# Queries and keys of the forgetting heads by one level of Strassen, late values with tokens stationary, and an inverse rms spread by DMA

## The chip, the cores and the metric

The kernel runs on one core of one Trainium2 chip. The metric is the device time of one execution in microseconds (us); the time before is the median of three runs. The core has five engines that each take their own instructions in order: TensorE (PE in the profile, its weight loads apart as PEld), VectorE (DVE), ScalarE (ACT), GpSimd (POOL) and SyncE (SP). SP computes nothing here; it issues nearly all DMAs, one after the other, and an issue that must wait for a buffer holds those behind it. Engines wait for each other by semaphores.

## The reference, cut to what matters

One layer over 1024 tokens of width 1024, in float32. The part that the change touches is the input projection and what feeds from it:

```python
h = rmsnorm(x, g_mix_pre[l])
proj = h @ w_in[l]                      # 1024 x 3080
fq, fk, fv = ...                        # 8 forgetting heads of 64: 512 columns each
f_logit = proj[..., 1536:1544] + b_fgt  # one forget gate per forgetting head
cq, ck, cv = ...                        # 8 chunked heads of 64: 512 columns each
# forgetting attention: causal softmax of q.k/8 + cumulative sum of log sigmoid(f_logit)
# chunked attention: own chunk of 64 and 8 chunks before, with a relative bias
x = x + rmsnorm(concat(rmsnorm(y_fox), rmsnorm(y_chk)) @ w_out, g)
x = x + rmsnorm(memory_cross_attention(rmsnorm(x), rmsnorm(mem), w_mq, w_mk, w_mv, w_mo), g)
x = x + rmsnorm(square(relu(rmsnorm(x) @ w_ff1)) @ w_ff2, g)
```

## The kernel before

**Arithmetic.** Every float32 operand of a product is held as two rounded tiles, a high part (hi, the operand rounded by an ACT copy) and a low part (lo, operand minus hi, on DVE or POOL). A product is three matmuls, hi by hi, hi by lo, lo by hi (mm3, L174 to L176). The gain of the norm is multiplied into x^T when it is split (hT, L1590); the inverse rms of a token is multiplied in after the projection, from a tile rt that holds it along the free dimension, the same in all 128 partitions.

**Stages.** The opening (L1522 to L1709) is written out by hand in one order for all engines. Slabs of x^T for the first 512 tokens (half th=0) land together with 264 columns of value and gate weights (xw, L1542); as each lands, it is split and multiplied into the values of the first four forgetting heads, tokens stationary (value_rounds, L1633). Then come the values of the other forgetting heads, the second half of the tokens, and beside them the rms: the rows of x are squared on ACT with a running sum (L1600), POOL adds epsilon and takes the power -1/2 (root), DVE spreads that over a diagonal matrix (L1610, L1612), PE multiplies it with ones and ACT copies the result out as rt (spread, L1619, L1621). After the last value part the forget gates are worked out on DVE and ACT (forget_gates, L392 to L426), transposed on PE (ftr), summed by a scan on DVE (L424), and stored; the bias rows of the attention are loaded from there.

The attention (attention_phase) is laid out by a planner (Flow, L56 to L126). It holds streams of steps: values (pv), turns (transposes ptr), scores (sc), side steps, row norms, and last a filler. Step by step it takes the first stream whose next step has its operands and buffers by its own reckoning, and it orders DVE, ACT, POOL and the DMAs by due time and level. What it decides is fixed when the program is built. The filler (filler_steps, L1492) runs, for the eight pairs of heads (four forgetting, n=0 to 3, then four chunked, n=4 to 7), the projections of queries and keys with weights stationary, 512 tokens wide (project_steps, L681): a scaling by rt on DVE (L724), splits per head, and for keys copies by DMA to the other 64 partitions (L746). For chunked pairs it also makes values (vt) with weights stationary, which PE transposes later (vtr, L762 on). After these come the memory keys, the first half of the output projection (mix_steps(0)) and the memory values. Beside the planner, pumps issue loads when buffers come free: Stock (L262) the weights, Biases (L434) the bias rows, WeightSums (L913) loads w_mo during the attention, forms four differences of its blocks on DVE (L926) and stores them in DRAM (wt) for the memory's output projection, which already runs as a Strassen product. The feed-forward part after it (lines from L1709 on, with Block, HiLo, bank and product as helpers) does so too.

## Time and profile before

| what | value |
|---|---|
| median of 3 runs | 1453.06 us (1452.79 to 1455.76) |
| span of the profiled execution | 1451.2 us (the page prints no other time of it) |
| mean granted TensorE clock | 0.999 |
| opening, 0 to 60 us: PE, DVE, ACT, POOL busy | 58.95, 29.82, 40.65, 17.22 us; 225 GB/s |
| attention with projections, 60 to 440 us | 380.00, 279.57, 251.43, 179.56 us; 143 GB/s |
| attention, output projection and memory queries, 440 to 700 us | 259.52, 173.85, 160.17, 50.87 us; 183 GB/s |
| the rest, 700 us to the end | 744.92, 479.36, 371.01, 136.33 us; 192 GB/s |

A matmul is pipelined: its busy time in the profile (0.28 to 0.39 us) is longer than the step from one start to the next. What one costs is read from the starts. In lines of a timeline the columns are start, time, engine, line, operation, tiles (written <- read), shape and count; in brackets stands the idle time before and what ended it. Lines of waits end in three numbers: the sum, the count, the mean. A group line gives the busy time, the mean of one in ns, and the idle time before with its releasers. A line of DMA issues gives their count, the KB of each, and the median us from issue to landing.

### The profile page before, as it was taken

How to read it: one execution, taken by the hardware profiler on the slowest of the kernel's cores; microseconds unless marked ns; L12 is line 12 of the kernel's file. 1: busy time of each engine (PE TensorE's matmuls, PEld its weight loads, DVE VectorE, ACT ScalarE, POOL GpSimd, SP SyncE). 2: the span in 40 equal slices, each digit the busy share in tenths (PEclk: the TensorE clock that was granted, in tenths of full speed). 3: DMA queues.
4: the chain of work that ended last, by engine and by line, in shares of the span. 5: the costliest groups of instructions: out<-in, count | busy, mean ns of one | idle time of the engine just before them, and what ended most of it. 6: DMA issues, size and time to landing. Idle time of an engine off the chain costs nothing.

```text
span 1451.2 us, 20902 instructions
## 1 busy us (share of the span) xinstructions
PE 1443.4 (99%) x7252; PEld 1222.7 (84%) x7252; DVE 962.6 (66%) x1651; ACT 823.3 (57%) x1466; POOL 384.0 (26%) x454
## 2 busy tenths in 40 slices
PE   9999999999999999999999999999999999999998
PEld 9988888888889888888888888888888888888886
DVE  5567778867667546966685697655555766655576
ACT  7457776676577664566665455545555453444442
POOL 1345555444344102400021504333331000000021
PEclk9999999999999999999999999999999999999999
DMA  8233667854548766542352646754444775445565
GB/s 335 66 102 91 146 166 191 279 120 124 134 95 247 216 204 237 188 161 63 123 200 74 211 154 231 264 185 159 160 160 160 297 304 192 138 148 189 185 250 203
DMA packets 100970, 259.44 MB, mean 179 GB/s; under 512 B 12520, under 2 KB 25072, under 8 KB 100864
## 3 DMA queue, kind: packets, MB, share of 16 engines
q1 hardware_dynamic: 96112, 249.71, 51.3%
q0 software_dynamic: 4608, 8.39, 4.0%
q8 instruction: 57, 0.93, 0.3%
q14 instruction: 49, 0.40, 0.1%
q10 hardware_dynamic: 144, 0.00, 0.0%
HBM read 181.98 MB, written 76.08 MB: 178 GB/s over the span
## 4 chain that ended last, share of the span: by engine, by line
PE 98%; DVE 0%; DMA 0%; ACT 0%; issue 0%; SPq 0%; DVEq 0%; POOLq 0%; POOL 0%; ACTq 0%
PE pv L638 4%; PE fx L175 4%; PE fx L174 4%; PE fx L176 4%; PE ptr L588 4%; PE px L176 3%; PE fy L174 3%; PE px L175 3%; PE fy L175 3%; PE px L174 3%; PE fy L176 3%; PE yw L174 2%; PE q L174 2%; PE q L176 2%; PE q L175 2%; PE mq L174 2%
## 5 line engine op out<-in xcount | busy, mean ns | idle before, releaser
L594 DVE TENSOR_TENSOR p<-ptr,p 128x512 fp32r<-128x512 f32 (+1 forms) x152 | 92.5, 616 | 29.4 <-ACT p L597 28.5
L2102 ACT ACTIVATE whif<-ra 128x1024 fp32r<-128x1024 f32 x37 | 39.2, 1061 | 126.2 <-PE fy L175 62.6
L2104 DVE TENSOR_TENSOR wlof<-ra,whif 128x1024 fp32r<-128x1024 f32 x37 | 45.3, 1225 | 88.7 <-ACT whif L2102 88.7
L597 ACT ACTIVATE p<-ptr 128x512 fp32r<-128x512 f32 (+1 forms) x152 | 79.9, 538 | 41.7 <-PE ptr L588 40.8
L2216 POOL TENSOR_SCALAR rf<-sf 128x1 f32<-128x1 f32 x8 | 8.2, 1030 | 324.7 <-ACT jf L2201 324.5
L638 PE MATMUL pv<-p,vs 128*128 128x512 f32 (+1 forms) x304 | 86.3, 371 | 0.0
L174 PE MATMUL fx<-vhif,whif 128*128 128x512 f32 x168 | 65.4, 389 | 0.0
L176 PE MATMUL fx<-vhif,wlof 128*128 128x512 f32 x168 | 65.4, 389 | 0.0
L175 PE MATMUL fx<-vlof,whif 128*128 128x512 f32 x168 | 65.4, 389 | 0.0
L638 PEld LDWEIGHTS pv<-p,vs 128*128 128x128 f32 x304 | 53.4, 189 | 8.7 <-DVE p L594 0.2
L1991 POOL TENSOR_TENSOR sc<-wf,wf 128x512 f32<-128x512 f32 x14 | 21.7, 1553 | 144.1 <-DMA wf<-in_w_ff 144.1
L174 PE MATMUL k<-hT_hi,whik 128*128 128x512 f32 x128 | 52.6, 411 | 0.0
L174 PE MATMUL mq<-h2T_hi,whimq 128*128 128x512 f32 x128 | 51.6, 403 | 0.0
L174 PE MATMUL q<-hT_hi,whiq 128*128 128x512 f32 x128 | 51.0, 398 | 0.0
L174 PE MATMUL yw<-whiwo,yT_hi 128*128 128x512 f32 x128 | 50.6, 395 | 0.0
L175 PE MATMUL k<-hT_lo,whik 128*128 128x512 f32 x128 | 50.2, 393 | 0.0
L176 PE MATMUL k<-hT_hi,wlok 128*128 128x512 f32 x128 | 50.2, 392 | 0.0
L176 PE MATMUL q<-hT_hi,wloq 128*128 128x512 f32 x128 | 50.1, 391 | 0.0
L176 PE MATMUL mq<-h2T_hi,wlomq 128*128 128x512 f32 x128 | 50.1, 391 | 0.0
L175 PE MATMUL q<-hT_lo,whiq 128*128 128x512 f32 x128 | 50.1, 391 | 0.0
L175 PE MATMUL mq<-h2T_lo,whimq 128*128 128x512 f32 x128 | 50.0, 391 | 0.0
L176 PE MATMUL yw<-whiwo,yT_lo 128*128 128x512 f32 x128 | 49.9, 390 | 0.0
(673 smaller groups left out, 4941.1 us busy)
## 6 DMA issues: line engine op xcount, KB each, us to landing
ra<-gd SPq DMA_DIRECT2D x56, 512.0 KB, 3.7
wg<-in_w_ff SPq DMA_DIRECT2D x56, 512.0 KB, 5.0
wf<-in_w_ff SPq DMA_DIRECT2D x38, 512.0 KB, 4.0
gd<-s SPq DMA_DIRECT2D x48, 256.0 KB, 2.1
od<-ot SPq DMA_DIRECT2D x64, 128.0 KB, 2.7
od<-od POOLq DMA_DIRECT2D x32, 256.0 KB, 4.9
wrawmq<-in_w_mq SPq DMA_DIRECT2D x16, 512.0 KB, 3.9
gd<-u SPq DMA_DIRECT2D x32, 256.0 KB, 2.0
```

The costliest lines, as they stand in the source:

```text
L174: nc.tensor.matmul(ps, lh, rh, start=start, stop=False, skip_group_check=more)
L175: nc.tensor.matmul(ps, lh, rl, start=False, stop=False, skip_group_check=more)
L176: nc.tensor.matmul(ps, ll, rh, start=False, stop=stop, skip_group_check=more)
L588: nc.tensor.transpose(tr[:, m, :], sp[:, k * P:(k + 1) * P], ident)
L594: flow.put("V", at, 0.56 if dead else 0.7, lambda: nc.vector.tensor_sub(pl[:, live, :], tr[:, live, :], f(ph[:, live, :])), done)
L597: flow.put("S", flow.end, 0.49 if dead else 0.6, lambda ph=ph, tr=tr, live=live: nc.scalar.activation(ph[:, live, :], tr[:, live, :], AF.C ...
L638: nc.tensor.matmul(pv[:, :, q0 * P:(q0 + k1 - k0) * P], v, x[:, :, k0:k1, :].rearrange("p m k q -> p m (k q)"), start=c == 0 and m == 0, s ...
L1991: eng.tensor_sub(sc[:, k1], r0[:, k0], r1[:, k0])
L2102: nc.scalar.activation(ah, ra, AF.Copy)
L2104: nc.vector.tensor_sub(al, ra, f(ah))
L2216: nc.gpsimd.tensor_scalar(r, ssf[b][:, 0:1], ssf[b][:, 1:2], EPS, op0=ALU.add, op1=ALU.add)
```

## The change

**Queries and keys of the four forgetting pairs move into the opening (NS = 4).** With x^T cut into quarters, B11 and B21 (first 512 tokens, first and second half of the width) and B12 and B22 (the second 512 tokens), and the weights of one pair into four blocks (query and key, first and second half of the width), the four result blocks (query and key, each for two halves of tokens) are made of seven products instead of eight, each 12 matmuls of 128x512. Two of the seven need only raw weights and first-half slabs: the slabs now bring the query weights of all four pairs (x_wq0, L1544), and as they land the products with B11 (firsts) and B21 (seconds) run, 12 matmuls for each slab (L1628). The first goes to DRAM, as does the sum of both, named g11 (second_out, L1602 to L1606, tiles part1). The other operands are sums of quarters of the normed x^T: POOL norms (L1609), DVE forms T1 and T2 (L1660, L1661), POOL T3 and T4, and `turned` splits T2, T1, T3, T4 and B22 (L1654, L1655). The rows of x have two buffers now, and the square of one issues the load of the row two behind (L1582). Then a class Pair loads a pair's raw query and key weights (wq, wk, L1560), forms three weight sums sc, r1 and sd (L1725 to L1729), on DVE for the first pair and on POOL for the others, and splits them (L205, L208; tiles v, w and u, with s23, s1a and s4 in their names). Per pair five products follow (x with T2, z with T1, x with T3, v with T4, z with B22), and `emit` multiplies by rt, splits and stores a query's or key's hi and lo half to DRAM (qkd, L1768 to L1779). The attention loads them from there, three tiles of a head by six DMAs (class Heads, L530).

**The values of the forgetting heads come after the pairs.** B12 is loaded again and split (L1856 to L1861), the value weights come in their own loads (w_v0, w_v1), and four value parts follow, all their matmuls as before. Between them stand the weight differences of w_mo (weight_sums replaces WeightSums), the gates, their transposes, scan and store, which were side steps before, the first loads of queries and keys, and the first bias rows.

**The inverse rms is spread by DMA.** `root` stores the 512 inverse rms of a half as 512 elements in DRAM (rdr, L1591) and loads them back to all partitions (rt0, rt1, L1592). The diagonal, its matmuls and the copy go.

**Late values with tokens stationary.** The values of the chunked pairs are made two pairs at a time, 256 columns wide and tokens stationary (late_value_steps), without transposes. Projections of the chunked pairs (project_steps) store their halves in DRAM too. Memory values stand ahead of mix_steps(0) in the filler, and buffer counts and levels of the planner follow.

Three places show how instructions move; the number at the end of a name is a running number of the tile. On SP, at the end of the opening's loads, there stood before the last rows of x, two small loads, and the first query and key weights of the attention:

```order
L1562 DMA x_4_397<-in_x 128x1024 [waits DMAHW5_49,Activation_49]
L1562 DMA x_5_399<-in_x 128x1024 [waits DMAHW6_49,Activation_49]
L1562 DMA x_6_401<-in_x 128x1024 [waits DMAHW7_49,Activation_49]
L1562 DMA x_7_403<-in_x 128x1024 [waits DMAHW0_49]
L1678 DMA bfgt_85<-in_b_fgt 128x8 [waits DMAHW1_49]
L1679 DMA gcol_86<-in_g_heads 128x8 [waits DMAHW2_49]
L310 DMA wrawq_0_407<-in_w_qk 128x1024 [waits DMAHW3_49,DVE_49]
L310 DMA wrawk_0_409<-in_w_qk 128x1024 [waits DMAHW4_49,DVE_49]
```

Now, from the last store of part1 to the weights of the first pair:

```order
L1605 DMA part1_3_147<-xw7_216 128x512 [waits DMAHW1_49]
L1606 DMA part1_3_147<-g11_3_453 128x512 [waits DMAHW2_49,DVE_49]
L1554 DMA x_5_474<-in_x 128x1024 [waits DMAHW3_49,Activation_49]
L1554 DMA x_6_477<-in_x 128x1024 [waits DMAHW4_49,Activation_49]
L1591 DMA rdr_143<-rall_88 128x4x1 [waits DMAHW5_49,Pool_49]
L1592 DMA rt0_89<-rdr_143 128x512 [waits DMAHW6_49,DMAHW5_49]
L1554 DMA x_7_496<-in_x 128x1024 [waits DMAHW7_49,Activation_49]
L1560 DMA wq0_512<-in_w_qk 128x1024 [waits DMAHW0_49]
L1560 DMA wk0_514<-in_w_qk 128x1024 [waits DMAHW1_49]
```

The two weight loads stood behind rows of x before as well; now the stores, the write of the inverse rms and its load back stand among the rows, with waits for DVE, ACT and POOL, and wq0 and wk0, which the first pair's products need, stand behind all of them.

On ACT, from the squares of the second half of the rows on, there stood the value copies (vs), the copy of rt, and the high part of the first query weight of the attention:

```order
L1600 ACTIVATE junk6_609,ss41_222<-x_6_401 128x1024 [waits DMAHW7_49,Activation_49]
L1600 ACTIVATE junk7_611,ss41_222<-x_7_403 128x1024 [waits DMAHW0_49,Activation_49]
L1647 ACTIVATE vs1_0_201<-v100_245,rall_88 128x4x64
L1647 ACTIVATE vs1_0_201<-v101_246,rall_88 128x4x64
L1621 ACTIVATE rt1_671<-rt1_668 128x512 [waits PE_49]
L323 ACTIVATE whiq_0_779<-wrawq_0_407 128x1024 [waits DMAHW3_49]
L323 ACTIVATE whik_0_784<-wrawk_0_409 128x1024 [waits DMAHW4_49]
```

Now, from the square of x_5 (two splits of T4 and one of B22 are left out here):

```order
L1582 ACTIVATE x_5_474,ss41_243<-x_5_474 128x1024 [waits DMAHW3_49,Activation_49]
L1582 ACTIVATE x_6_477,ss41_243<-x_6_477 128x1024 [waits DMAHW4_49,Activation_49]
L1582 ACTIVATE x_7_496,ss41_243<-x_7_496 128x1024 [waits DMAHW7_49,Activation_49]
L1654 ACTIVATE T4_hi0_500<-xw4_210 128x512 [waits Pool_49]
L1654 ACTIVATE T4_hi1_501<-xw7_216 128x512 [waits Pool_49]
L1654 ACTIVATE hT1k2_hi0_238<-xt12_220 128x512 x2
L1654 ACTIVATE hT1k2_hi1_239<-xt13_224 128x512
L205 ACTIVATE vhi_s230_542<-qsc0_534 128x1024 [waits DMAHW5_49,DVE_49,Activation_49]
L205 ACTIVATE whi_s1a0_546<-wk0_514 128x1024 [waits DMAHW1_49]
```

The splits of T4 and B22 stand between the squares and the first pair's weight split vhi_s230, which the first product of that pair, PE's row after the slab products, reads.

On DVE, around the start of the gates (fz is the gate's logit), the value parts' low halves were followed by the gates at once:

```order
L1650 SCALAR_TENSOR_TENSOR vs0_2_199<-v010_533,rall_88,vs0_2_199 128x4x64 [waits PE_49,Activation_49]
L1650 SCALAR_TENSOR_TENSOR vs0_3_200<-v013_536,rall_88,vs0_3_200 128x4x64 [waits PE_49,Activation_49]
L397 TENSOR_TENSOR fz_773<-fcol_144,bfgt_85 128x8 [waits DMAHW1_49]
L397 TENSOR_TENSOR fz_773<-fcol_144,bfgt_85 128x8 x7
L401 TENSOR_SCALAR fl_775<-fz_773 128x64 [waits DVE_49]
```

Now the second four differences of w_mo stand ahead of the last value part's low halves and of the gates:

```order
L948 TENSOR_TENSOR wm111_1099<-wm121_1100,wm111_1099 128x1024 [waits DMAHW6_49,DMAHW5_49]
L948 TENSOR_TENSOR wm121_1100<-wm221_1102,wm121_1100 128x1024 [waits DMAHW7_49,DVE_49]
L948 TENSOR_TENSOR wm221_1102<-wm221_1102,wm111_1099 128x1024 [waits DVE_49]
L948 TENSOR_TENSOR wm211_1101<-wm211_1101,wm221_1102 128x1024 [waits DMAHW0_49,DVE_49]
L1892 SCALAR_TENSOR_TENSOR vs0_2_1085<-v010_1236,rall_88,vs0_2_1085 128x4x64 [waits PE_49,Activation_49]
L1892 SCALAR_TENSOR_TENSOR vs0_3_1086<-v013_1239,rall_88,vs0_3_1086 128x4x64 [waits PE_49,Activation_49]
L429 TENSOR_TENSOR fz_1348<-fcol_1082,bfgt_85 128x8 [waits DMAHW2_49]
L429 TENSOR_TENSOR fz_1348<-fcol_1082,bfgt_85 128x8 x7
L433 TENSOR_SCALAR fl_1350<-fz_1348 128x64 [waits DVE_49]
```

All eight differences left the attention for this place, each with waits for its own loads.

The diff, cut to its core:

```diff
+    NS = 4
+    VS = {5: 2, 7: 3}
...
-    class WeightSums:
...
+    def weight_sums(k):
+        raw = {n: u4(f"wm{n}{k}", (P, 2, HT), F32) for n in ("11", "12", "21", "22")}
+        for n, (a, b) in (("12", (0, 1)), ("11", (0, 0)), ("22", (1, 1)), ("21", (1, 0))):
+            nc.sync.dma_start(raw[n], mo(a, b, k))
+        def sums():
+            for n, to, a, b in (("T1", "11", "12", "11"), ("T3", "12", "22", "12"), ("T2", "22", "22", "11"), ("T4", "21", "21", "22")):
+                nc.vector.tensor_sub(raw[to], raw[a], raw[b])
+                nc.sync.dma_start(wt[n][k], raw[to])
+        return sums
...
-        for n in range(8):
-            part = all_of(("qk", n), 12)
-            for ths in ((0,), (1,)) if n == 0 else ((0, 1),):
-                yield from project_steps("q", n, part, ths)
-                if n > 3:
-                    yield from project_steps("v", n, part)
-                yield from project_steps("k", n, part, ths)
+        for n in range(NS, 8):
+            yield from project_steps(n)
+            if n in VS:
+                yield from late_value_steps(VS[n])
...
+            r = pa.tile([P, D], F32, tag="xr", bufs=2, name=f"x_{b}")
...
+            nc.scalar.activation(xrow[b], xrow[b], AF.Square, scale=1.0 / 32.0, accum_out=ssx[b // 4][:, b % 4:b % 4 + 1])
+            if b + 2 < TB:
+                load_row(b + 2)
...
-            d = p1.tile([P, 2, 4, P], F32R, tag="ph", bufs=2, name=f"diag{th}")
...
+            row = rdr[th:th + 1, :]
+            nc.sync.dma_start(bass.AP(tensor=row.tensor, offset=row.offset, ap=[[1, P], [P, 4]]), r)
+            nc.sync.dma_start(rt[th], row.to_broadcast([P, HT]))
...
+            g = pa.tile([P, HT], F32, tag="t2", bufs=3, name=f"g11_{n}")
+            nc.vector.tensor_add(g, ps, p1t[n])
+            nc.sync.dma_start(part1[n][:, 0, :], p1t[n])
+            nc.sync.dma_start(part1[n][:, 1, :], g)
...
+            to = seconds if kc > 3 else firsts
...
+                for n in range(4):
+                    nc.tensor.matmul(to[n], a[:, n * P:(n + 1) * P], b, start=kc % 4 == 0 and m == 0, stop=kc % 4 == 3 and m == 2)
...
+            nc.vector.tensor_sub(T1[kc], xt1[kc], T1[kc])
+            nc.vector.tensor_sub(T2[kc], xt1[kc + 4], T1[kc])
...
+            nc.gpsimd.tensor_sub(T3[kc], xt1[kc + 4], T3[kc])
+        for b in range(3):
+            square(b)
...
+            turned("T2", kc, T2[kc])
+        for n in range(4):
+            second_out(n, seconds[n])
...
+            nc.gpsimd.tensor_sub(T4[kc], T2[kc], T4[kc])
+        for kc in range(4):
+            turned("T1", kc, T1[kc])
...
+        for b in range(3, 5):
+            square(b)
+        root(0)
+        for kc in range(4):
+            turned("T3", kc, T3[kc])
...
+        for b in range(5, 8):
+            square(b)
+        for kc in range(4):
+            turned("T4", kc, T4[kc])
...
+                eng.tensor_sub(sc[:, k1], r0[:, k0], r1[:, k0])
+                eng.tensor_add(r1[:, k0], r1[:, k0], r1[:, k1])
+                eng.tensor_sub(sc[:, k0], r1[:, k0], r0[:, k0])
...
+                eng.tensor_sub(sd, r0[:, k1], sc[:, k0])
...
+        cur, nxt = Pair(0), Pair(1)
+        cur.load("q")
+        cur.load("k")
+        root(1)
+        for kc in range(4):
+            turned("B22", kc, xt1[kc + 4])
...
+        cur.sums(nc.vector)
+        nxt.load("q")
+        for name in ("s23", "s1a", "s4"):
+            cur.split(name)
...
+            product(x, w["s23"], 0, XT["T2"])
...
+            product(z, w["s1a"], 0, XT["T1"])
...
+            product(x, w["s23"], HT, XT["T3"], more=True)
...
+            product(v, w["s1a"], HT, XT["T4"])
...
+            product(z, w["s4"], 0, XT["B22"], more=True)
...
+        wsums = weight_sums(0)
...
+        wsums()
+        wsums = weight_sums(1)
+        value_part(0, 0, vals)
...
+        wsums()
+        value_part(0, 1, vals)
         gparts, gate_turn, gate_scan, gate_store = forget_gates()
...
+        value_part(1, 0, w1)
+        nc.sync.dma_start(rd, rows[0])
+        turn, out_ = gate_turn
+        for g in range(2):
+            turn(g)
+        for g in range(2):
+            out_(g)
+        gate_scan()
+        gate_store()
+        for _ in range(2):
+            for call in qkheads.loads()[1]:
+                call()
+        biases.first()
+        value_part(1, 1, w1)
+        stock.split_now(1)
```

More of the change, by code (lines that the diff above doesn't have):

```diff
@@ L795, in side_steps @@
+            if g == 3 and kb == 3:
+                for _ in range(8):
+                    free["u4"].give(flow.end)
+        for i in range(2):
+            stock.done(("wv", g, i))
+    def side_steps():
         mT = Act("mT", NM)
-        mem_in.append(mT)
+        mem_T.append(mT)
         for k in range(0, KC, 2):
@@ L1596, in build @@
+        xt1 = xt1[0:2] + xt1[4:6] + xt1[2:4] + xt1[6:8]
+        for n in range(4, min(7, NS)):
+            wq[n] = qk_raw(n, "q")
+        for b in range(2):
+            load_row(b)
+        hT = [Act("hT0"), Act.__new__(Act)]
+        hT[1].per = 2
+        B11 = Block("", (hT[0].h[0:2], hT[0].l[0:2]))
+        B21 = Block("", (hT[0].h[2:4], hT[0].l[2:4]))
+        B22 = Block("hT1k2")
+        XT = {}
         ssx = [small.tile([P, 4], F32, tag="ss4", bufs=2, name=f"ss4{th}") for th in range(2)]
@@ new lines, in build @@
+        last = lambda: None
+        for n in range(NS):
+            more = n + 1 < NS
+            after = Pair(n + 2) if n + 2 < NS else None
+            w = cur.w
+            if more:
+                nxt.sums()
+                reload(n + 1)
+            both = saved.pop(n)
+            p1, g11 = both[:, 0, :], both[:, 1, :]
+            x = bank(f"qx{n}")
+            product(x, w["s23"], 0, XT["T2"])
+            u2 = t2q(f"qu2_{n}")
+            nc.vector.tensor_add(u2, x, p1)
+            last()
+            low = emit(n, "q", 0, g11)
+            if after:
+                after.load("q")
+            elif more:
+                value_load(0)
+            else:
+                value_load(2)
+            z = bank(f"qz{n}")
+            product(z, w["s1a"], 0, XT["T1"])
+            low()
+            if more:
+                nxt.split("s23")
+            else:
+                value_split(0)
+            product(x, w["s23"], HT, XT["T3"], more=True)
+            u3, g22 = t2q(f"qu3_{n}"), t2q(f"qg22_{n}")
+            nc.vector.tensor_add(u3, x, p1)
+            nc.vector.tensor_add(g22, z, u3)
+            emit(n, "k", 1, g22, nc.gpsimd)()
+            v = bank(f"qv{n}")
+            product(v, w["s1a"], HT, XT["T4"])
+            if more:
+                nxt.split("s1a")
+                if after:
+                    after.load("k")
+                else:
+                    value_load(1)
+            else:
+                value_split(1)
+                value_split(2)
+            nc.vector.tensor_sub(u3, u3, v)
+            emit(n, "k", 0, u3, nc.gpsimd)()
+            product(z, w["s4"], 0, XT["B22"], more=True)
+            if more:
+                nxt.split("s4")
+            nc.vector.tensor_add(u2, z, u2)
+            last = emit(n, "q", 1, u2)
+            cur, nxt = nxt, after
@@ new lines, in build @@
+        last()
+        B12 = Block("hT1k1")
+        for kp in range(2):
+            xr = wp.tile([P, 2, HT], F32, tag="wraw", bufs=3, name=f"xr{kp}")
+            nc.sync.dma_start(xr, t["x_t1"][kp])
+            for j in range(2):
+                kc = kp * 2 + j
+                h, l = B12.at(kc)
+                nc.scalar.activation(h, xr[:, j, :], AF.Copy, scale=gp[:, kc:kc + 1])
+                nc.vector.scalar_tensor_tensor(l, xr[:, j, :], gp[:, kc:kc + 1], f(h), op0=ALU.mult, op1=ALU.subtract)
```

683 lines of the change are left out of this document (347 added, 336 removed).

## The prediction

> **What bounds the kernel now.** I read the page's busy line first, then its slices, its chain, and last the waits of TensorE alone.
>
> ```profile
> span 1451.2 us, 20902 instructions
> ...
> PE 1443.4 (99%) x7252; PEld 1222.7 (84%) x7252; DVE 962.6 (66%) x1651; ACT 823.3 (57%) x1466; POOL 384.0 (26%) x454
> ...
> PE   9999999999999999999999999999999999999998
> ...
> PE 98%; DVE 0%; DMA 0%; ACT 0%; issue 0%; SPq 0%; DVEq 0%; POOLq 0%; POOL 0%; ACTq 0%
> ```
>
> ```profile
> PE warm L1528 <- DVE o L196: 1.0, 1, 1.0
> PE sc6g L515 <- DVE mnc6g L519: 0.5, 1, 0.5
> ```
>
> PE is 98% of the chain, and its only waits of note are 1.0 us at the start and 0.5 us in the middle. So two things move the time: the matmuls that go or come, and every gap in PE, each one for one. The page gives no time of the profiled execution beside its span; the median of the runs, 1453.06, stands 1.9 us above it, and I add my sum to the median.
>
> **Matmuls.** Starts, not durations, give a pipelined matmul's price.
>
> ```profile
> 699.73 0.39 PE L176 MATMUL mq<-h2T_hi,wlomq 128*128 128x512 f32 x1
> ...
> 703.81 0.39 PE L176 MATMUL ym<-whimo,A11l 128*128 128x512 f32 x1
> ```
>
> ```profile
> 19.01 0.28 PE L174 MATMUL v<-whiv,hT_hi 128*128 128x256 f32 x1
> ...
> 28.96 0.28 PE L176 MATMUL v<-whiv,hT_lo 128*128 128x256 f32 x1
> 29.08 0.62 PE L1619 MATMUL rt<-diag,ones_r 128*128 128x512 f32 x2
> 29.54 0.28 PE L174 MATMUL v<-whiv,hT_hi 128*128 128x264 f32 x1
> ```
>
> ```profile
> 100.34 0.87 PE ptr L588 x8
> ```
>
> From the first to the last of the 19 wide matmuls are 18 steps in 4.08 us: 0.2267 us each. The 84 of 256 columns take 9.95 us in 83 steps: 0.120. A transpose is 0.87/8 = 0.109; a pair for rt takes 0.46.
>
> - Queries and keys of the four forgetting pairs: 4 x 96 = 384 wide matmuls become 4 x 84 = 336 (seven products of 12 instead of eight). 48 x 0.2267 = **10.9 us saved**.
> - Late values: 192 wide and 32 transposes (43.5 + 3.5) become 384 of 256 columns (46.0): **1.0 saved**.
> - rt by DMA: four matmuls go, **0.9 saved**.
>
> Together -12.8 us. All other PE work is the same in number and shape.
>
> **The seam.** The opening now runs 96 of the 336 matmuls (the products with B11 and B21) as the slabs land, and then PE's next row is qx0<-T2,vhi_s230, in order, with nothing ahead of it. I lay the queues out to it with these rows:
>
> ```profile
> 8.69 0.65 PE L1633 MATMUL v<-whiv,hT_hi 128*128 128x264 f32 x4
> ```
>
> ```profile
> 17.26 1.06 ACT L1600 ACTIVATE junk<-x 128x1024 bf16<-128x1024 f32 x1 [0.41 <-DMA x<-in_x]
> ...
> 18.61 1.06 ACT L1600 ACTIVATE junk<-x 128x1024 bf16<-128x1024 f32 x1 [0.19 <-DMA x<-in_x]
> ...
> 25.91 2.60 ACT L1590 ACTIVATE hT_hi<-xf,gp 128x512 fp32r<-128x512 f32 x4
> 29.74 0.60 ACT L1621 ACTIVATE rt<-rt 128x512 f32<-128x512 f32 x1 [1.23 <-PE rt L1619]
> 30.24 2.55 ACT L1590 ACTIVATE hT_hi<-xf,gp 128x512 fp32r<-128x512 f32 x4
> ...
> 42.30 1.05 ACT L323 ACTIVATE whiq<-wrawq 128x1024 fp32r<-128x1024 f32 x1
> ```
>
> ```profile
> L329 DVE TENSOR_TENSOR wlomq<-wrawmq,whimq 128x1024 fp32r<-128x1024 f32 x12 | 14.7, 1221 | 2.1 <-ACT whimq L323 1.8 <-PE mq L175 0.3
> ...
> L724 DVE TENSOR_TENSOR kn<-k,rt 128x512 f32<-128x512 f32 x16 | 11.0, 689 | 14.1 <-PE k L176 14.1
> ```
>
> ```profile
> gd<-s SPq DMA_DIRECT2D x48, 256.0 KB, 2.1
> ...
> wrawk<-in_w_qk SPq DMA_DIRECT2D x8, 512.0 KB, 3.6
> ```
>
> ```profile
> gp<-in_g_pre ACTq DMA_DIRECT2D x1, 4.0 KB, 2.9
> bfgt<-in_b_fgt SPq DMA_DIRECT2D x1, 4.0 KB, 9.2
> ```
>
> PE's second slab starts at 8.69 in before; 120 KB more lie ahead of it now, so 9.0. Seven slabs of 12 x 0.2267 end at **28.0**: each slab lands sooner than PE needs it, because the two x rows landed 1.35 us apart per 512 KB.
>
> Row x_0 landed at 17.2 behind 4128 KB; now 6144 KB lie ahead: 5.3 us later, 22.5, x_1 at 23.9. The rows have only two buffers, so x_2 is issued when ACT has squared x_0 (23.6) and lands 3.6 later, 27.2. ACT is in order: square of x_2 to 28.3, the high parts of T2 and T1 (8 x 0.65) to 33.5, squares of x_3 and x_4 to 35.7, T3 to 38.3. On DVE the low parts of T2 end at 31.6; the first g11 is added by 32.3, its store lands at 34.5 (2.1), and the fourth g11 waits for that buffer: 35.2. SP holds the fourth store until then; behind it stand x_5 (issued 35.7, landed 39.4), x_6, the write of the inverse rms (rdr, 36.8, +2.9), rt0, x_7 (needs the square of x_5: 40.6), and only then wq0 and wk0. Those land at 1.35 us each behind x_7 (44.2): 46.9. ACT squares x_7 to 45.3, then T4 and B22 (8 x 0.65) to 50.5; DVE's last low part 51.2, its three weight sums (3 x 0.69) 53.3, vhi 1.05, vlo 1.22: the third matmul of qx0 may start at 55.6. Less the two that run before it, PE stands from 28.0 to 55.1: **27 us**. Bounds: ACT splits at 0.50 (the next starts 0.50 after the 0.60 us copy above) take 3 to 4 off: 23. The write rdr moves 512 elements of 4 bytes, which no row shows; 2.9 is the small idle-queue load, 9.2 the one behind traffic, which would hold SP 6 us longer: 33. I take 2.9, since here few loads are ahead.
>
> The Trainium skill, "DMA: Bandwidth & Descriptors", Specifications, says transfers under 512 B cost a read-modify-write; no row of before tests that on a 4-byte write, and it would push towards 33.
>
> **The restart.** How PE runs after a stop is shown only at the start:
>
> ```profile
> 4.74 1.25 PE L1633 MATMUL v<-whiv,hT_hi 128*128 128x264 f32 x4
> 5.78 1.08 PE L1633 MATMUL v<-whiv,hT_lo 128*128 128x264 f32 x4
> 6.66 0.76 PE L1633 MATMUL v<-wlov,hT_hi 128*128 128x264 f32 x4
> 7.26 0.63 PE L1633 MATMUL v<-whiv,hT_hi 128*128 128x256 f32 x4
> ```
>
> The first twelve took 2.52 us, the next twelve 1.43. PE had run since 1.05, so some 5.6 us were slow; at half speed they lose 2.8. I take **2**, between 0 and 2.8. "TensorE: Matmul & The Clock Gate" of the Trainium skill (Why this matters for your kernels) wants no PE gap over about 3 us, since the clock then halves for about 3.4 us: by it the term would be 1.7 and no other term changes. It speaks against this change.
>
> **The pairs.** Per pair PE has 60 matmuls, 13.6 us; DVE twelve 512-wide operations and two of 1024, 10.7 us, hidden. POOL has six:
>
> ```profile
> 43.43 2.54 POOL L332 TENSOR_TENSOR wloq<-wrawq,whiq 128x512 fp32r<-128x512 f32 x2 [5.03 <-ACT whiq L323]
> ```
>
> at 1.27, 7.6 us. But the next key weight is queued on SP behind a key store that waits for POOL's low part, so from the end of x's second product run: two sums, scale, split, low (4), load (3.6), wait for the second low, three weight sums, high and low (8), u3 and g22 (1.4): about 17 against PE's 16.3. Half a microsecond in three of the pairs: **1.5**, between 0 and 5 (POOL slower).
>
> **The gates.** The late part of the opening, counted from the end E of the last pair:
>
> ```profile
> 46.83 2.06 DVE L397 TENSOR_TENSOR fz<-fcol,bfgt 128x8 f32<-128x8 f32 x8
> ...
> 53.35 0.22 DVE L410 SCALAR_TENSOR_TENSOR fe<-fz,fe 128x64 f32<-128x64 f32 x1
> 53.50 1.65 DVE L1650 SCALAR_TENSOR_TENSOR vs<-v,rall,vs 128x256 fp32r<-128x256 f32 x4
> ...
> 61.95 2.28 DVE L424 TENSOR_TENSOR_SCAN fla<-fea 8x1024 f32<-8x1024 f32 x1 [0.29 <-ACT fea L421]
> ```
>
> ```profile
> L926 DVE TENSOR_TENSOR wm<-wm,wm 128x1024 f32<-128x1024 f32 x8 | 10.7, 1338 | 0.1
> ```
>
> PE has three value parts, E+34.7, then the gate transposes. Ahead of the gates DVE now does the eight weight differences of w_mo, in order with their loads: SP gets to x_t1 again at E+3.2; wv11 waits for a buffer (8.9); four w_mo loads end at 17.9, DVE's four differences at 20.5, four value splits 22.2. The next four loads stand behind the stores: landed 28.7, differences 31.4, splits 33.0, and the gate chain of 6.7 us ends at 39.7. PE waits **5** (0 to 9). After it, scan, store, twelve reloads and the bias rows end about 1 us after PE's fillers: **1** (0 to 3).
>
> **Attention.** Four pairs' projections no longer fill PE there, but their scalings and copies left DVE too:
>
> ```profile
> 180.00:240.00 60.00, 60.00 (x323) 50.80 (x322) 47.55 (x116) 41.83 (x85) 36.57 (x51) 1.00 0.72 185
> ```
>
> DVE has 79% of this stretch. Per forgetting pair 96 matmuls (21.8 us of PE) and about 9 us of DVE go; chunk pairs lose 4 us of DVE each. So DVE stays under 80% of PE, and I take **1** (-0.5 to 8).
>
> Sum: -12.8 + 27 + 2 + 1.5 + 5 + 1 + 1 = +24.7, so **1478 us**.
>
> **Rivals.** *The seam is covered.* If wq0 and wk0 landed before 28 us and ACT reached the split at once, the seam and the restart go: -12.8 + 8.5, **1449 us**. It decides below 4.3 us of seam and restart together. For it: DMA could carry these 1024 KB in 2.7 us. Against: eight rows of x stand ahead on SP with two buffers. 0.03. *Shorter seam, quiet gates*: 23 + 2 and nothing else, **1465**; 0.15. *Starved attention or a slow rdr*: PE waits there as in no stretch of before, or SP loses 6 us: +14, **1492**; 0.18. For it: attention loses its filler. *The matmuls do not go* can be excluded; they are counted in the built order.
>
> The forecast has 0.62 and its own range 1468 to 1488; 0.02 is left for no change. The range reaches to the two near rivals, 1463 to 1494. A measurement tells about 0.2% from none. Faster 0.03, same 0.02, slower 0.95.
>
> **What would show it.** A PE gap of over 20 us from about 28 us, released by ACT vhi_s230; slow first matmuls after it; a short wait of ftr on DVE; attention without gaps. PE's idle line near zero would make all this wrong; so would a gap ended by DMA alone before 40 us.

## The result, and the profile after

The changed kernel takes 1557.66 us, the median of four runs (1554.65 to 1561.73), against 1453.43 for the kernel before (four runs, 1452.79 to 1455.76): 1.0718 times as long, with an interval of 1.0699 to 1.0737. That is 104 us more, where 25 were forecast. The profiled execution has 1557.5 us and a span of 1555.7.

From the page after: the span, PE's busy line, PE's slices (each 38.9 us) and the chain.

```profile
span 1555.7 us, 21445 instructions
...
PE 1453.8 (93%) x7360; PEld 1230.2 (79%) x7360; DVE 995.4 (64%) x1665; ACT 819.6 (53%) x1466; POOL 405.5 (26%) x480
...
PE   6188889999998899999999999999999999999998
...
PE 75%; DMA 7%; DVE 3%; issue 2%; POOL 2%; ACT 1%; SPq 0%; POOLq 0%; DVEq 0%; ACTq 0%
```

Before, every slice but the last stood at 9 and PE was 98% of the chain. Now the second slice is nearly empty, and the four after it and two in the attention stand at 8. PE's waits by releaser, the largest six:

```profile
PE qx L174 <- ACT vhi_s L205: 44.4, 1, 44.4
PE qx L174 <- DVE qu L1812: 7.5, 4, 3.1
PE pv L709 <- DVE p L668: 7.2, 4, 4.6
PE ftr L449 <- DVE fe L442: 6.1, 1, 6.1
PE sf0g L589 <- DVE mnf0g L593: 4.7, 1, 4.7
PE qz L174 <- DVE qg L1831: 4.3, 3, 1.5
```

Waits are not all. A table by stage needs what PE took and what its matmuls are worth: I gave each matmul its price from the prediction (0.2267 us for 512 columns, 0.12 for 256, 0.109 for a transpose, other shapes by their own steady steps) and took the sum from the time between the starts, counted from PE's first start. What is left over is waits and slow clock.

| stage, up to the first … | before: price + left over | after: price + left over | left over, after less before |
|---|---|---|---|
| opening (score of a forgetting head) | 78.2 + 3.5 | 124.9 + 77.8 (63.4 of it waits) | 74.3 |
| forgetting attention (chunked score) | 197.7 + 3.1 | 174.8 + 16.9 | 13.8 |
| chunked attention (memory keys) | 157.6 + 1.9 | 111.8 + 10.9 | 9.0 |
| memory keys and end of attention (output projection) | 40.2 + 0.9 | 75.5 + 11.9 | 11.0 |
| the rest | 958.4 + 2.4 | 932.4 + 11.4 | 9.0 |

The price falls by 12.7 us in all, the left over grows by 117.1; together 104.4, the difference of the two spans (104.5).

**The seam.** SP's queue in it (start, time in issue, line, transfer):

```profile
27.31 0.42 SPq L1605 DMA_DIRECT2D part<-xw  x1
37.53 0.33 SPq L1606 DMA_DIRECT2D part<-g  x1
...
41.39 1.35 SPq L1554 DMA_DIRECT2D x<-in_x  x2
42.83 0.43 SPq L1591 DMA_DIRECT2D rdr<-rall  x1
54.72 0.34 SPq L1592 DMA_DIRECT2D rt<-rdr  x1
55.15 0.38 SPq L1554 DMA_DIRECT2D x<-in_x  x1
```

SP stood 10 us for the first g11, and then 11.9 us for one write of 512 elements of 4 bytes, since the load of rt must see it landed; x_7 waited behind both. The same write for the second half of the tokens came when nothing else moved:

```profile
64.60 0.38 SPq L1591 DMA_DIRECT2D rdr<-rall  x1
73.79 0.33 SPq L1592 DMA_DIRECT2D rt<-rdr  x1
```

It held its load for 9.2 us. The DMA engines moved 528 packets of 4 bytes between 65.50 and 65.88 us and nothing else until 73.79. In the first write, which shared the engines with two rows of x, the last packet ended at 47.99, and the load was issued 6.7 us later. So more than half of the 11.9 us is a delay behind the last packet, and what the traffic ahead adds is about the 2.7 by which the first hold is longer. (In the seven other runs with this write the two holds are 9.1 to 10.5 and 7.8 to 8.1 us.)

ACT and PE then went on as forecast, but late:

```profile
61.96 1.06 ACT L1582 ACTIVATE x<-x 128x1024 f32<-128x1024 f32 x1 [12.55 <-DMA x<-in_x]
...
70.70 1.06 ACT L205 ACTIVATE vhi_s<-qsc 128x1024 fp32r<-128x1024 f32 x1 [3.44 <-issue]
```

```profile
71.81 0.79 PE L174 MATMUL qx<-T_hi,vhi_s 128*128 128x512 f32 x1 [44.44 <-ACT vhi_s L205]
...
77.48 0.40 PE L174 MATMUL qz<-T_hi,whi_s1a 128*128 128x512 f32 x1
...
83.44 0.50 PE L174 MATMUL qx<-T_hi,vhi_s 128*128 128x512 f32 x1 [3.07 <-DVE qu L1812]
...
84.24 0.59 PE L174 MATMUL qx<-T_hi,vhi_s 128*128 128x512 f32 x1
...
87.89 0.39 PE L174 MATMUL qv<-T_hi,whi_s1a 128*128 128x512 f32 x1
```

From 71.81 to 77.48 are twelve matmuls in 5.67 us, worth 2.72: the restart costs 2.95. A gap of 3.07 us is then enough for a second slow stretch, nine matmuls from 84.24 in 3.65 us. The six gaps of 1.2 to 1.6 us in the pairs bring none. But a long gap is not the only way into one: from 159.2 to 162.7 us matmuls of 264 columns start every 0.22 us instead of 0.12 (granted clock 0.50 from 160 to 162), and in the 3 us before no two starts lie more than 0.91 us apart.

**The attention.** Windows of its three stages, after and before (stretch, length, busy time and count of PE, PEld, DVE, ACT, POOL, granted clock, DMA share, GB/s):

```profile
203.70:395.40 191.70, 180.62 (x1060) 155.89 (x1059) 121.63 (x356) 122.25 (x257) 98.21 (x158) 0.99 0.73 189
395.40:518.10 122.70, 115.84 (x741) 104.41 (x740) 82.64 (x258) 84.31 (x194) 57.41 (x86) 0.97 0.85 225
518.10:605.50 87.40, 81.04 (x509) 72.19 (x507) 63.05 (x149) 61.62 (x122) 28.25 (x34) 0.96 0.78 211
```

```profile
82.70:283.00 200.30, 200.30 (x1082) 169.50 (x1081) 158.37 (x398) 140.20 (x288) 111.04 (x165) 1.00 0.58 154
283.00:443.00 160.00, 160.00 (x882) 137.57 (x882) 111.44 (x303) 105.68 (x223) 67.37 (x90) 1.00 0.54 132
```

DVE fell from 79% to 63% of the first stretch, as forecast, and it made no difference. What rose is the DMA share, from 0.58 and 0.54 to 0.73 and 0.85. The bias rows (biasf, biasc) and the memory's key weights now take longer from issue to landing; the last column of the DMA issues, after and before:

```profile
biasf<-cd SPq DMA_DIRECT2D x8, 512.0 KB, 7.7
...
wrawmk<-in_w_mk SPq DMA_DIRECT2D x8, 512.0 KB, 7.0
...
biasc<-rd SPq DMA_DIRECT2D x8, 320.0 KB, 8.0
```

```profile
biasf<-cd SPq DMA_DIRECT2D x8, 512.0 KB, 4.9
...
wrawmk<-in_w_mk SPq DMA_DIRECT2D x8, 512.0 KB, 3.8
...
biasc<-rd SPq DMA_DIRECT2D x8, 320.0 KB, 3.7
```

Not every load got slower: the blocks of w_out (wrawwo) landed after 7.8 us before and 5.3 now. The planner goes on reckoning with the short landings. One place where that ends in a stop of PE (4.63 us at 474): a load that must wait for its own store holds SP, the first block of w_mk stands behind it, and ACT, in order, waits for that block ahead of the copies that PE needs.

```profile
462.09 5.22 SPq L877 DMA_DIRECT2D memn<-md  x2
...
467.86 0.58 SPq L342 DMA_DIRECT2D wrawmk<-in_w_mk  x1
```

```profile
475.66 1.06 ACT L355 ACTIVATE whimk<-wrawmk 128x1024 fp32r<-128x1024 f32 x1 [7.92 <-DMA wrawmk<-in_w_mk]
```

### The profile page after: what moved, and what is told of

It is laid out like the page before. It is cut to its first block, busy times and chain, and to the rows that moved or that the text cites. A ratio compares the mean times of both kernels' runs of the same rounds, so it can differ in the third digit from the quotient of the medians.

```text
span 1555.7 us, 21445 instructions
## 1 busy us (share of the span) xinstructions
PE 1453.8 (93%) x7360; PEld 1230.2 (79%) x7360; DVE 995.4 (64%) x1665; ACT 819.6 (53%) x1466; POOL 405.5 (26%) x480
## 4 chain that ended last, share of the span: by engine, by line
PE 75%; DMA 7%; DVE 3%; issue 2%; POOL 2%; ACT 1%; SPq 0%; POOLq 0%; DVEq 0%; ACTq 0%
PE fx L175 4%; PE fx L176 4%; PE fx L174 4%; PE pv L709 3%; PE fy L176 3%; PE fy L175 3%; PE fy L174 3%; PE px L176 3%; PE px L175 3%; PE px L174 3%; PE ptr L662 3%; DMA biasf<-cd 2%; PE pz L174 2%; PE pz L176 2%; PE pz L175 2%
## 5 line engine op out<-in xcount | busy, mean ns | idle before, releaser
L174 PE MATMUL qx<-T_hi,vhi_s 128*128 128x512 f32 x32 | 14.7, 460 | 51.9 <-ACT vhi_s L205 44.4
L174 PEld LDWEIGHTS qx<-T_hi,vhi_s 128*128 128x128 f32 x32 | 6.8, 213 | 55.3 <-ACT vhi_s L205 44.9
L175 PE MATMUL yw<-wlowo,yT_hi 128*128 128x512 f32 x128 | 49.9, 390 | 0.0
L175 PE MATMUL fy<-vlof,whif 128*128 128x512 f32 x128 | 49.9, 390 | 0.0
L176 PE MATMUL fy<-vhif,wlof 128*128 128x512 f32 x128 | 49.9, 389 | 0.0
L174 PE MATMUL fy<-vhif,whif 128*128 128x512 f32 x128 | 49.8, 389 | 0.0
```

The costliest lines, as they stand in the source:

```text
L174: nc.tensor.matmul(ps, lh, rh, start=start, stop=False, skip_group_check=more)
L175: nc.tensor.matmul(ps, lh, rl, start=False, stop=False, skip_group_check=more)
L176: nc.tensor.matmul(ps, ll, rh, start=False, stop=stop, skip_group_check=more)
```

## The experiments

The runs of the changed kernel are 7 us apart, so a single time below decides nothing under some 5 us; where less is at stake, the trace's rows or the stage's left over decide. Times without a range are of one run. The runs that leave the seam as it is have a gap of 41.9 to 43.3 us there, the profiled run of the changed kernel 44.4, so 1 to 2.5 us of each difference to it lie in the seam.

### The seam

**The inverse rms by diagonal and PE again.**

```diff
-            nc.sync.dma_start(bass.AP(tensor=row.tensor, offset=row.offset, ap=[[1, P], [P, 4]]), r)
-            nc.sync.dma_start(rt[th], row.to_broadcast([P, HT]))
+            nc.tensor.matmul(ps, ones_r, d[:, m].rearrange("p a b -> p (a b)"), start=m == 0, stop=m == 1)
...
+            nc.scalar.activation(rt[th], ps, AF.Copy)
```

> One part undone: the inverse rms is spread by a diagonal and PE again, without the 4-byte store (rdr) and its load back; all else as in the changed kernel. Theory SP order: in the changed kernel SP stood 11.9 us, 42.8 to 54.7, for rdr to land, with x_7, wq0 and wk0 behind it, and the first pair then stood again because its part1 reload was issued behind the second rdr (73.8). So PE's long gap (44.4 us) falls to 31 to 35 us, the 3.1 us gap before the second product of the first pair goes, and the time falls by 12 to 18 us, to 1540 to 1546. Rival, ACT and DVE splits set the end of the gap: it stays within 3 us of 44.4 and the time within 4 us of 1557.

1543.62 us, 14 less. The gap falls from 44.4 to 32.65 us, with 2.39 behind it:

```profile
60.10 0.80 PE L1604 MATMUL rt<-diag,ones_r 128*128 128x512 f32 x1 [32.65 <-DVE diag L1595]
...
66.17 0.80 PE L174 MATMUL qx<-T_hi,vhi_s 128*128 128x512 f32 x1 [2.39 <-ACT vhi_s L205]
```

The first score of the attention starts 12.2 us sooner (191.5 for 203.7 us). So the DMA spread, which was to save 0.9 us, cost about 12 in the opening; the other 2 are no more than runs differ by.

**The same, and the stores of part1 behind the first pair's weights** (the fourth g11 gets a buffer of its own).

```diff
-            nc.sync.dma_start(part1[n][:, 0, :], p1t[n])
-            nc.sync.dma_start(part1[n][:, 1, :], g)
...
         cur.load("q")
         cur.load("k")
+        for n in range(4):
+            part_store(n)
```

> The run with the rms by PE (e5, 1543.6 us), and beside it the stores of part1 stand on SP behind the first pair's weights instead of ahead of x_5. In e5 SP stood from 28.6 to 38.2 for the first g11, and x_5 to x_7 landed at 47.6 to 52.6. Theory SP holds: the rows land 7 to 9 us sooner, PE's gap (27.1 to 60.1 and to 66.2) ends 7 to 9 us sooner, and the time is 1534 to 1537. Rival, DVE is the limit of this stage by now (its low parts took 1.7 us each while POOL worked, 0.62 without): under 3 us less than e5.

1531.56, 12.1 less than the run above and under the 1534 to 1537 expected. The gap is 24.1, 8.6 less, and the first score starts 7.9 us sooner (183.6): that much the stores' place on SP had cost. The other 4 us lie in the attention, which this edit doesn't touch. So the theory of SP's holds is right for both, and 24 us of gap are left.

**POOL taken out of the way.** On top of all mends below (e13), the differences T3 and T4 go from POOL to DVE, and four of the eight scalings of x^T to ACT.

```diff
-            nc.gpsimd.tensor_sub(T3[kc], xt1[kc + 4], T3[kc])
+            nc.vector.tensor_sub(T3[kc], xt1[kc + 4], T3[kc])
```

> As e13, and in PE's gap the eight differences T3 and T4 move from POOL to DVE, and four of the eight scalings of the second half of x^T from POOL to ACT. In e11 DVE's four low parts of T2 took 1.70 us each while POOL's differences ran (1.57 each), and 0.62 each later with POOL still. Theory, the two slow each other: DVE takes 5.5 us more work, but the low parts fall to 0.62 (4.3 less), T1's to 0.62 (1.1 less), and the scalings end 4 us sooner, so the gap in PE ends 3 to 6 us sooner than in e13. Rival, the low parts were slow for their own sake: they stay at 1.7, and the gap ends 3 to 6 us later.

1514.54 against 1515.16, no difference; the gap is 22.2 us instead of 24.1 and ends 1.2 us sooner, where 3 to 6 were expected. But DVE's low parts of T2 show why g11 came late. First after, DVE and POOL; then this kernel's DVE:

```profile
30.11 6.79 DVE L1655 TENSOR_TENSOR T_lo<-xw,T_hi 128x512 fp32r<-128x512 f32 x4
```

```profile
28.39 6.29 POOL L1669 TENSOR_TENSOR xt<-xt,xt 128x512 f32<-128x512 f32 x4
```

```profile
30.51 2.49 DVE L1674 TENSOR_TENSOR T_lo<-xw,T_hi 128x512 fp32r<-128x512 f32 x4
```

Beside POOL's subtractions each of the four takes 1.70 us, alone 0.62. The additions of g11 that follow, with one operand in PSUM (the matmuls' output banks), took 0.62 each although POOL's next subtractions ran beside them. The Trainium skill, "SBUF — State Buffer" (SBUF: two separate sides), says DVE operations with two operands in SBUF and GpSimd's share a pair of ports under an exclusive lock held for a whole instruction; that agrees.

**The first pair's weights ahead of the rows of x**, and its first two products ahead of the spread.

```diff
+        raw0 = {w: qk_raw(0, w) for w in "qk"}
         for b in range(2):
             load_row(b)
...
+                z = bank(f"qz{n}")
+                product(z, w["s1a"], 0, XT["T1"])
+                for th in range(2):
+                    spread(th, diags[th], "tr")
```

> The kernel of e15_pool_out (1514.54 us; gap of 22.2 us and then 2.4 us) with the raw weights of the first pair loaded ahead of the rows of x, their sums and splits made beside those of T2 and T1, and the products with T2 and T1 (24 matmuls, 5.4 us) run before the rms is spread. Theory A (the seam is a matter of order: what stands in the gap is there to be done): 5.4 us of matmuls and the 2.4 us wait leave the part behind the gap, the rows of x land some 2.7 us later, so 1508 to 1511. Theory B (the seam is bounded by ACT and DVE, which have no time left between 28 and 52 us; the weight work only pushes the splits of T3 and T4 back by as much): 1513 to 1517.

1519.68 (1517.69 to 1524.93; 1.046, interval 1.0435 to 1.0486): 5 us more, worse than either theory. The single gap became three, of 10.7, 11.9 and 4.1 us:

```profile
PE rt L1605 <- DVE diag L1596: 13.0, 2, 11.9
PE qx L174 <- ACT vhi L205: 10.7, 1, 10.7
PE qx L174 <- DVE qu L1847: 4.1, 1, 4.1
```

DVE shows why the first of them cannot go by loading sooner:

```profile
26.97 2.49 DVE L1689 TENSOR_TENSOR xt<-xt,xt 128x512 f32<-128x512 f32 x4
30.20 2.50 DVE L1675 TENSOR_TENSOR T_lo<-xw,T_hi 128x512 fp32r<-128x512 f32 x4 [0.74 <-ACT T_hi L1674]
32.62 2.47 DVE L1619 TENSOR_TENSOR g<-qx,xw 128x512 f32<-128x512 f32 x4
35.01 0.68 DVE L1709 TENSOR_TENSOR qsc<-wq,wk 128x512 f32<-128x512 f32 x1
```

From the last slab on, DVE works nearly without a pause until the first pair's weights are summed; PE starts at 38.28 at the earliest. The time that the two products gain is lost again on x_7, squared only at 51.5, and on part1, which now comes back late. In the orders tried the seam is work of DVE and ACT as well as waiting.

### The pairs

The splits of the next pair's weights each one product later, so that DVE reads the full bank first.

```diff
             low()
-            if more:
-                nxt.split("s23")
...
             product(v, w["s1a"], HT, XT["T4"])
             if more:
-                nxt.split("s1a")
+                nxt.split("s23")
```

> In the loop over the four pairs the weight splits of the next pair stand later on DVE and ACT: the split of s23 behind the reads of z, that of s1a behind the reads of v, that of s4 in the next pair. Same instructions in number. Theory: PE waited 1.4 to 1.6 us twice per pair because the second product of x and of z accumulates into a bank that DVE must read first, and DVE stood in order behind a low part that waited for ACT's high part. Seven of the eight waits go (the first, 3.1 us, is a DMA's): 8 to 10 us less. Rival: the sums on POOL are late, so the splits wait anyway and the gaps come back at the first product of the next pair: under 3 us less.

1551.96, 5.7 less, under the 8 to 10 expected. The waits for qu and qg fall from 11.8 us to 3.1 (1.5 and 1.6), but 2.3 on the low part of s1a and some under 1 us come in their place. The opening's left over is 5.4 less, of which 2.1 lies in the seam, which this edit doesn't touch: about 3 us are the pairs'. That PE waited for DVE to empty a bank is shown; that these waits can be ordered away in full is not.

### The gates

Three runs: the subtractions of w_mo left out; the gate's bias loaded early; both.

```diff
-                nc.vector.tensor_sub(raw[to], raw[a], raw[b])
...
+        nc.sync.dma_start(bfgt, t["b_fgt"].to_broadcast([P, 8]))
+        nc.sync.dma_start(gcol, t["g_heads"])
         B12 = Block("hT1k1")
```

> The eight weight differences of w_mo are left out on DVE (the loaded blocks are stored as they are, so the memory's output projection gets other weights); all loads and stores stay. Theory: the gate transposes waited 6.1 us (183.2 to 189.3) because the gate chain on DVE stood behind these differences, which stand behind their own loads. The wait falls under 1 us and the time by 5 to 8 us (6.1 of idle and up to 1.5 of a slow restart). Rival: the gate's own chain of 5 us after the last gate logits sets it, and more than 4 us of wait stay.

> The 4 KB load of the gate's bias (bfgt) and gcol are issued ahead of the loads for the late part of the opening; the differences of w_mo stay on DVE. In the run without the differences (e3) DVE stood 9.8 us for bfgt, issued at 171.0 behind the eight w_mo loads, landed at 179.2, and the wait of the gate transposes stayed (5.7 us). Theory, two holds side by side: the differences alone hold DVE until 182, so the wait stays at 5 to 6.5 us and the time within 3 us of 1557. Rival, bfgt alone was the cause: wait under 1 us, 5 to 8 us less.

> Both at once: bfgt early, and the differences of w_mo left out on DVE (the memory's output projection gets other weights). Theory, two holds side by side, each of which hides the other: now the gates start when their logits are copied (about 172) and end 6 us later under the value part that runs to 183; the wait of the gate transposes is under 0.5 us and the time falls by 5 to 8 us. Rival, a third hold stands behind these: over 3 us of wait stay.

Without subtractions 1557.79, and PE's wait for the gates stays. DVE, freed, stands for another load, the gate's own bias, issued behind those of w_mo:

```profile
179.19 0.71 DVE L429 TENSOR_TENSOR fz<-fcol,bfgt 128x8 f32<-128x8 f32 x8 [9.75 <-DMA bfgt<-in_b_fgt]
```

So the theory that the differences alone make the wait fell. With the bias early alone 1556.77, wait 6.6; with both 1548.07, and the wait is gone: 9.6 less, of which 2.5 are the seam's, so the 5 to 8 expected. Two holds end at about the same time: taking one away shows nothing.

### The attention

**The twelve loads of queries and keys ahead of the value part,** so that the first bias rows stand alone behind the gate's store.

> The first twelve loads of queries and keys for the attention are issued ahead of the value part of the second half, so that the first two bias rows stand alone behind the gate store; nothing else moves. Theory: the first score waited for its bias row, issued 8.3 us after the gate store (202.8 against 194.5) behind twelve issues of 0.6 us each and landing 10.3 us later, behind their 3 MB. Now issued by 196 and landed 5 to 6 us later, so the first score's output is scaled by 203, not 213, PE's idle of 4.7 us at 209 goes and the slow restart with it: 6 to 10 us less. Rival: the chain of gates, scan, store and broadcast sets it: under 2 us less.

1545.82, 11.8 less, more than the 6 to 10 expected. After, the bias rows were issued at 202.82, 8.6 us after the store they read, and used 10.4 after that; DVE, after:

```profile
213.23 0.69 DVE L593 CUSTOM_DVE_ANT_0 spf0g<-sf0g,biasf 128x512 f32<-128x512 f32 x1 [8.31 <-DMA biasf<-cd]
```

With the edit the rows are issued at 198.66 and used at 202.81: 4.2 us. They are still issued 6.5 us after their store (192.11), whose landing SP now waits for. So of the 8.3 us gained here 2.1 are the twelve issues, and 6.2 are the landing behind their 3 MB. PE's wait for the first score is gone, and the left over of the three attention stages falls from 39.7 to 31.6.

**The planner reckons 3.5 us more for each landing.**

```diff
-        self.put("D", at, 0.55, call, then and (lambda end: then(end + took)))
+        self.put("D", at, 0.55, call, then and (lambda end: then(end + took + 3.5)))
```

> The planner reckons 3.5 us more from the issue of a DMA to its landing, everywhere in the attention and the stage behind it; no work is added. In the changed kernel bias rows land after 7.7 us and keys after 6.5 to 7.0, where the planner has 4.5 and 4.0. From 222 to 600 us PE lost 31 us (17 idle, the rest slow clock behind the gaps) against 6 in the same work before. Theory, the plan puts PE's and ACT's steps where the operands are not there yet: with true landings the steps between are filled by projections, and 10 to 20 us of it go. Rival, the projections that filled it are gone or used up, so the same idle time moves elsewhere: within 5 us of 1557.

1541.55, 16 less. The three stages fall from 39.7 to 27.7, with the same matmuls; the opening, which the planner doesn't lay out, gives 2.6 of the 16. So a good part of the loss was in the plan, and a plan with later landings takes it away. That the longer landings had made the old plan bad is argued from the landings above; no run shortens them.

**The first block of w_mk ahead of the memory's rows as well.**

```diff
-            self.blocks += ["norm", "mem"]
+            self.blocks += ["norm", mk[0], "mem"] + mk[1:]
```

> The kernel of e7_landing (planner reckons 3.5 us more for each landing, 1541.55 us) with the first block of w_mk loaded ahead of the two loads of the memory's normed rows, instead of behind them. There ACT waited 6.18 us for wrawmk, whose load stood on SP behind a load that was held 4.84 us for its own store, and PE stopped 4.2 us at 466. Theory (what is left of the attention's loss after e7 is queue order on SP, a load behind a held one): the stop goes, 1537 to 1539. Rival (the attention is short of work to overlap, whatever the loads do): another stop takes its place, 1541 to 1543.

1532.1 (1530.01 to 1536.67; 1.0535, interval 1.0516 to 1.0554); its profiled run, 1536.67, stands 4.9 under the one run of e7. The median lies under both expectations. The stop at 466 falls from 4.2 us to one of 2.3 at 472, and the stages from 27.7 to 21.3. The stop had been queue order on SP, more than a lack of work. Before, the same stages had 5.9: some 15 us stay unexplained by one cause.

### All together

All mends at once (rms on PE, stores late, later splits, gate's bias and heads early, planner's landings), with the second differences of w_mo behind the first bias rows (e11) or behind the gate's chain (e13).

```diff
             call()
+        wsums()
         bias_rows(1)
...
         biases.first()
-        wsums()
```

> All mends in one kernel, the full result computed: rms by PE, part1 stores behind the first pair's weights, pair splits moved, bfgt early, the second four w_mo differences behind the gate store and the first bias rows, first head loads early, 3.5 us more landing time in the plan. Theory, separate places whose losses add: 1531.6 (rms and stores) - 5.7 (pairs) - 11.7 (heads early) - 9.5 (gates) - 12 (landing, less what it shares with the heads) = 1490 to 1497 us. Rival, they share a limit behind them (DMA supply or DVE), so that one mend uncovers the next wait: over 1505 us. In either case it stays slower than the kernel before, since the gap in PE from 27 us on is only shortened.

> The kernel with all mends (e11, 1522.4 us) again, but the second four w_mo differences stand behind the gate chain on DVE and ahead of the third value part, not behind the first bias rows. In e11 PE stood 10.3 us at the start of the attention: ACT's value copies of the last part waited 11.7 us for the late stores of those differences, whose buffers they take. Theory, that was the only collision: the wait goes and the sum of the single mends holds, 1505 to 1512 by e11 less 10 to 17 (wait and slow restart), 1490 to 1497 if all of them add. Rival, they share a limit: the wait comes back at another place and the time stays over 1515.

1522.37 and 1515.16, where the single savings added up to 1490 to 1497. So they don't add, as the rivals said (over 1505, over 1515), the second only just. In e11 the late stores of the differences held buffers that ACT's value copies write into, and PE stopped 10.3 us at the start of the attention:

```profile
186.50 0.84 ACT L1914 ACTIVATE vs<-v,rall 128x256 fp32r<-128x256 f32 x2 [11.74 <-DMA wtT<-wm]
```

In e13 4.2 of that are left, beside the gap of 24.1 us, 2.4 behind it, and 5.7 at the memory keys. There ACT waits 7.66 us for the first block of w_mk, the hold that e16 takes away and that these kernels still have.

**Six pairs instead of four** (without the late stores), to fill the seam with more slab products.

```diff
-    NS = 4
+    NS = 6
```

> The same without the moved part1 stores, and with six pairs instead of four by Strassen (the first two chunked pairs too): 24 matmuls of 0.2267 fewer (5.4 us), and their 48 products with B11 and B21 (10.9 us of PE) stand in PE's gap. Theory, the gap is what costs: it is filled by 10.9 us, the matmuls go, and only the two extra rounds of the pair loop and the thinner attention (no projections for two more pairs) cost some 5 us: 1480 to 1492. Rival, the extra weights (two more query slabs to load and split ahead of the others on ACT and DVE, where T1 and T2 wait too) push the first pair's products out by as much as they fill: 1497 or more.

1540.49, the rival's case (1497 or more). PE now works to 39.2 us, but the gap behind is still 25.9 us long and ends at 65.2, where it ended at 60.1 with four pairs and the stores in the same place (e5): what follows the slabs moved along with them. And the attention has less work of PE beside it:

```profile
PE rt L1605 <- DVE diag L1596: 25.9, 1, 25.9
PE sf0g L589 <- DVE mnf0g L593: 12.6, 3, 10.2
```

The left over of its forgetting attention is 37.6 us, where e11, with four pairs, has 15.7. So a lack of matmuls to fill in costs as well. No version came near the kernel before; the best, 1514.54, is 61 us slower. The mends together with e16's were not run.

## Why the prediction was wrong, step by step

The sign, the rival excluded and the saving held: 12.8 us of matmuls forecast, 12.7 measured. All that the range missed lies in the losses.

| term | forecast | measured | from |
|---|---|---|---|
| seam | 27 | 44.4 | wait for vhi_s |
| pairs | 1.5 | 11.8 | waits for qu and qg |
| gates | 5 | 6.1 | wait for fe |
| slow clock in the opening | 2 | 10.9 | 77.8 - 63.4, less 3.5 before |
| start of the attention and attention | 2 | 33.8 | three stages of the table |
| after the attention | 0 | 9.0 | table |

- **The seam, as a mechanism, was right**: it begins at 27.4, ends by vhi_s, and x_7 behind SP's holds sets its end. Three sizes were wrong. x_5 was to be issued at 35.7 and was at 41.4 (5.7): the step "low parts of T2 end at 31.6" took the duration of a DVE alone, and they ended at 36.9 beside POOL. The write rdr was taken at 2.9, the load on an idle queue, and took 11.9 (9.0). The step that failed there is the choice between a row with idle engines and a row with traffic: the second write took 9.2 us with idle engines, so the kind of write sets the hold, and no row of before has that kind. That the far bound, 9.2 us of a load behind traffic, equals the second hold is luck. x_7 was squared 6.8 us after its issue, not 3.6 (3.2). These 17.9 make the 17.4 missing, less half a microsecond that shorter steps give back. The rule cited from "DMA: Bandwidth & Descriptors" of the Trainium skill, on transfers under 512 B, pushed the right way; that a read-modify-write is what delays the landing, no run here shows.
- **The restart** cost 2.95, against 2 with a bound of 2.8. What failed is counting one stop: the pairs, the gates and the first score bring more stops of 3 us and over, each with its slow stretch, and one more slow stretch, at 159.2 us, comes without such a stop. The page of the Trainium skill cited there, "TensorE: Matmul & The Clock Gate", wants no gap over about 3 us, and the trace agrees that 3.07 is enough; its 3.4 us of slow clock are 3.65 after that gap, but 5.67 after the long one, and the stretch at 159.2 us is none that its rule foresees.
- **The pairs** failed in their first sentence: busy sums of PE and DVE (13.6 and 10.7 us) were compared, and DVE's called hidden. The second product of a pair adds into a bank that DVE must read first, and DVE, in order, stood behind low parts and reloads. A sum of busy times can't show that; the order of DVE's rows at that place does.
- **The gates** had the right size for half the reason: the differences, and also the gate's bias behind the loads of w_mo, which I passed by.
- **The attention** failed in its choice of resource. DVE's share was watched and fell. By their bytes it is the queries and keys of all pairs, now through DRAM, that took the DMA engines from 0.58 to 0.73 (in the three stages 84 loads and 32 stores of 256 KB stand where 56 copies of 128 KB stood; 82 MB in all instead of 63), and the bias rows' landings went from 5 and 4 us to 8; no run takes this traffic away. That "twelve reloads and the bias rows end about 1 us after PE's fillers" left out that the rows land behind the reloads' 3 MB (6.2 us, by e4) and are issued behind their twelve issues (2.1).
- **The rivals** "starved attention or a slow rdr" were one case with +14 us, one or the other. Both came, and not from one cause: the write was slow on idle engines too, and the attention lost time by its plan and by landings under traffic. The range was made as if terms missed one at a time.
- Of what would show it: the gap over 20 us, its releaser, the slow matmuls behind it and the wait of ftr on DVE all came; "attention without gaps" did not.

What stays open: some 15 us of the attention's loss and the 9 us behind it, for which no single place is large, and how short the seam could be in an order not tried.

## What to carry to other kernels

Before moving work from a place where it fills gaps to one where a chain must end first, write out the order of every queue at the new place and price each hold on it, a DMA whose result the same queue needs next above all; sums of busy time say nothing there. When a change adds DMA traffic, ask for each landing in the affected stages what it stands behind, and give a planner the new durations before judging the change. A wait with two causes shows nothing when one is taken away: try both, singly and together.

## What the runs showed of the hardware

- One DMA write of 512 separate elements of 4 bytes held the load that reads it for 11.9 us beside two loads of 512 KB, and for 9.2 us on idle engines, 7.9 of them behind its last packet.
- Subtractions on DVE with both operands in SBUF took 1.70 us each beside POOL's, 0.62 without; additions with one operand in PSUM took 0.62 beside POOL's too.
- After a stop of 3.07 us PE ran slow for 3.65 us, from 0.8 us after the restart; after one of 44.4 us, for 5.67 us at once; at 159.2 us it ran slow for 3.5 us with no two starts before it more than 0.91 us apart.
- Bias rows that landed in 4.9 us (at a DMA share of 0.58) and 3.7 us (0.54) took 7.7 (0.73) and 8.0 (0.85), while loads of w_out went from 7.8 to 5.3: the share alone doesn't give a landing.
